# One core, two blocks: values fetched a token at a time and summed on TensorE in four column groups; experts in line by count, with small passes early

## The chip, the cores and the metric

One core of one Trainium2 chip. The metric is the device time of one execution in microseconds, median of the timed runs; the kernel before takes 2327.17 us (three runs, 2323.35 to 2337.86).

## What is computed

256 tokens of 1024 numbers go through two blocks. The first ends in a product-key layer: each of 8 heads picks 16 of 16384 experts for a token, so a token has 128 choices; each choice is one row of `expert_u` and one of `expert_v`.

```python
act = jax.nn.gelu(jnp.einsum('td,thkd->thk', xt, expert_u[idx]))
return jnp.einsum('thk,thkd->td', g * act, expert_v[idx])
```

The second block ends in a mixture of 32 experts, four for each token, with a swiglu of 1024 columns; gate_up is 1024 x 2048 and down 1024 x 1024 of f32 for each expert, 12 MB:

```python
gu = xb @ w_gate_up[e] + b_gate_up[e]
act = (up + 1.0) * gate * jax.nn.sigmoid(1.702 * gate)
return act @ w_down[e] + b_down[e]
```

## The kernel before, in words

**The product-key layer** (`peer`, from L752). A loop over 128 tiles of `expert_u` (L133) leaves `prods`, every token's product with every row, in SBUF; `topk_steps` finds rows, weights and indices meanwhile. Then, in an order written out by hand:

`hot(n)` (L848) and `chosen(n)` (L860) handle four tokens: four bf16 matmuls (L854) and two ACT steps make a one-hot, four f32 matmuls (L864) pick 128 columns of `prods`, and four DVE operations (L867) sum out the one that counts. `act` then has one column for each token, 128 choices down the partitions. `weigh(tb)` (L871) transposes a block of 128 tokens, takes the Gelu and multiplies with the gates, giving `w` with tokens down the partitions.

The values are fetched by choice: `fetch_pair` (L830, L836) asks on the GpSimd queue for two transfers of 512 KB, each the n-th value row of all 128 tokens of a block. One of a pair is scaled and added on DVE (L895), the other on TensorE by a diagonal of weights that ACT makes (`make_dg` L886, `use_pair` L898: two matmuls of 128x128 weights and 512 columns). Ten such buffers ("homes") exist, five pairs: the three `raw` buffers and the places of two older tiles.

The order (L900 to L920) is: choose all 32 groups of block 0, weigh block 0, and only then use pairs; each second pair is followed by one group of block 1. After that `prods` is given up, and a late part (L969) uses the other 64 pairs in five new homes, while it loads four tiles of `w_in_2`, splits them on DVE, and closes block 0. The three `raw` buffers take the mixer's first loads (L1013) then. `close_block` (L952) adds the DVE sum to the TensorE sum, transposes and updates the residual.

**The experts** (`second` L1324, `moe` L1403). Loads of 1 MB, eight of gate_up and four of down for each expert, go out on SP in the order of `ORDER` (L40) into 16 slots and three places used once; `refill` (L1380) sends the next as soon as the slot's earlier content has been used, so PE's progress frees slots. SP takes its instructions in order.

A pass (L1650) gives an expert up to 64 tokens (`CAP`). Tokens are gathered by a one-hot product (`gather` L1448), two experts at a time. `gate_up` (L1495) is, for each of eight chunks of 128 rows, four matmuls: weights are 128 x 64 (the tokens), 512 columns move, two halves of the output columns stand side by side in the array (`tile_position`). `swiglu` (L1504) runs on DVE and ACT, `turn` transposes, `down` (L1520) is four chunks of four matmuls, `combine` (L1535) adds rows back to the tokens by four matmuls. While pass e runs gate_up, the down of pass e-1 is put between its chunks. `combine` and the sums share four PSUM banks `acc`.

There are 33 passes: the 32 experts as numbered, and one for the second 64 tokens of the fullest expert, whose weights are loaded again through an address read by SP (`value_load` L1655, L1362). `rank_experts` (L1598) finds it. Passes beyond that stand in a conditional (L1729) that runs only if more tokens are left over.

## Time and profile before

| | |
|---|---|
| median of the timed runs | 2327.17 us |
| the profiled execution's own time | 2305.36 us |
| its span | 2303.7 us |
| busy, share of the span | PE 89%, weight loads 55%, DVE 44%, ACT 28%, POOL 32% |
| DMA | 709.29 MB, mean 308 GB/s |
| mean granted TensorE clock | 0.965 |

A row of the timeline gives the start, the busy time, the engine, the line, the operation, output from inputs, and the count; in brackets the idle time before it and who ended it. PE records each f32 matmul twice (its two halves), so eight records are four matmuls. PE is matmuls, PEld the loading of their weights, POOL GpSimd, SPq the queue of SyncE. The granted clock is a share of 2.4 GHz.

### The profile page before, as it was taken

To read this page: it belongs to the slowest core of one execution; us is meant where nothing else is said; L and a number is where in the kernel's file an instruction comes from. 1 tells how busy PE (TensorE), PEld (TensorE's weight loads), DVE (VectorE), ACT (ScalarE), POOL (GpSimd) and SP (SyncE) were. 2 spreads that over 40 slices of the span, in tenths; PEclk is the share of its full clock that TensorE was granted. 3 is DMA by queue.
4 is the path that set the end of the run, shared out by engine and by line. 5 is a ranking of instruction groups with operands and counts; after the bars stand their busy time and mean duration, and the time that the engine had idled before them with its cause. 6 is when DMAs were issued, how large, how long until landed. Compare 5 with 4: busy or idle time off the path is not lost. (4 is left out here: it accounts for less than half of the span.)

```text
span 2303.7 us, 29592 instructions
## 1 busy us (share of the span) xinstructions
PE 2043.3 (89%) x11552; PEld 1256.2 (55%) x11552; DVE 1020.3 (44%) x2271; ACT 640.0 (28%) x1113; POOL 728.3 (32%) x498
## 2 busy tenths in 40 slices
PE   3878898998999889966779899999999999989986
PEld 2777888998999744422257433344444333333332
DVE  5988879994111767757556211111111111111112
ACT  4554343554555833311112111111111011100101
POOL 7454566885555167757730000000000000000000
PEclk7989999999999999989999899999999999999998
DMA  8346632454554279999957699999999999999996
GB/s 327 110 164 230 263 130 88 171 191 170 183 187 165 74 260 406 398 376 397 402 212 279 251 382 420 395 420 382 420 420 420 420 420 420 420 420 420 420 420 260
DMA packets 117892, 709.29 MB, mean 308 GB/s; under 512 B 13776, under 2 KB 14032, under 8 KB 48368
## 3 DMA queue, kind: packets, MB, share of 16 engines
q1 hardware_dynamic: 78192, 564.96, 61.5%
q0 software_dynamic: 36864, 134.23, 15.2%
q10 hardware_dynamic: 2688, 8.12, 1.0%
q8 instruction: 93, 1.52, 0.3%
q14 instruction: 55, 0.45, 0.1%
HBM read 706.21 MB, written 1.05 MB: 307 GB/s over the span
## 5 line engine op out<-in xcount | busy, mean ns | idle before, releaser
L1499 PE MATMUL ps_gu<-w,hgs 128*64 128x512 f32 x2104 | 497.4, 600 | 18.9 <-DMA w<-in_w_gate_up 18.9
L1781 POOL TENSOR_TENSOR xT<-xT,ple_w 128x512 f32<-128x512 f32 x1 | 1.3, 1261 | 1010.9 <-ACT xT L1771 1010.9
L1499 PEld LDWEIGHTS ps_gu<-w,hgs 128*64 128x64 f32 x2104 | 139.8, 137 | 286.7 <-issue 218.9
L111 POOL TENSOR_TENSOR wsl<-raw,wsh 128x1024 fp32r<-128x1024 f32 x104 | 253.7, 2442 | 132.1 <-PE ps_a L133 97.5
L1527 PE MATMUL ps_y<-w,mid 128*64 128x512 f32 x1048 | 248.2, 595 | 16.5 <-DMA w<-in_w_down 15.9
L898 PE MATMUL acc<-vp,dg 128*128 128x512 f32 x344 | 173.7, 634 | 55.0 <-DMA vp<-in_v,rows_late 28.6
L1465 DVE TENSOR_SCALAR hgs<-ps_hg,cols 128x128 f32<-128x128 f32 (+1 forms) x68 | 27.6, 406 | 335.4 <-PE ps_hg L1455 317.6
L1527 PEld LDWEIGHTS ps_y<-w,mid 128*64 128x64 f32 x1048 | 73.5, 137 | 174.0 <-issue 149.1
L133 PE MATMUL ps_a<-h2h,wsh 128*128 128x256 f32 x1024 | 146.2, 286 | 15.3 <-ACT prods L804 15.3
L1506 DVE TENSOR_SCALAR mid<-ps_gu 128x512 f32<-128x512 f32 x33 | 22.7, 686 | 290.3 <-PE ps_gu L1499 290.3
L898 PEld LDWEIGHTS acc<-vp,dg 128*128 128x128 f32 x344 | 62.2, 199 | 155.1 <-issue 79.6
L133 PE MATMUL ps_a<-h2h,wsl 128*128 128x256 f32 x1024 | 145.3, 285 | 0.0
L836 POOL DMA_INDIRECT vp<-in_v,rows_late x118 | 127.6, 1082 | 53.8 <-issue 24.4
L133 PE MATMUL ps_a<-h2l,wsh 128*128 128x256 f32 x1024 | 144.6, 284 | 0.0
L133 PEld LDWEIGHTS ps_a<-h2h,wsh 128*128 128x128 f32 x1024 | 133.9, 194 | 15.9 <-ACT prods L804 15.9
L108 ACT CAST wsh<-raw 128x1024 fp32r<-128x1024 f32 x128 | 136.8, 1068 | 6.2 <-DMA raw<-in_uT 6.0
L133 PEld LDWEIGHTS ps_a<-h2h,wsl 128*128 128x128 f32 x1024 | 133.7, 194 | 0.0
L133 PEld LDWEIGHTS ps_a<-h2l,wsh 128*128 128x128 f32 x1024 | 133.0, 193 | 0.0
L804 ACT COPY prods<-ps_a 128x256 f32<-128x256 f32 x128 | 80.2, 627 | 175.7 <-PE ps_a L133 164.5
L867 DVE SCALAR_TENSOR_TENSOR junk_p<-iota_i,i1T,ps_ch 128x128 bf16<-128x128 f32 x256 | 89.0, 348 | 68.1 <-PE ps_ch L864 58.0
L836 POOL DMA_INDIRECT raw<-in_v,top x84 | 85.8, 1022 | 86.9 <-DVE vsum L893 52.9
L1463 ACT ACTIVATE hgs<-ps_hg,cols 128x128 f32<-128x128 f32 (+1 forms) x68 | 30.9, 454 | 286.2 <-DVE hgs L1465 286.2
(504 smaller groups left out, 3184.9 us busy)
## 6 DMA issues: line engine op xcount, KB each, us to landing
w<-in_w_gate_up SPq DMA_DIRECT2D x263, 1024.0 KB, 19.8
w<-in_w_down SPq DMA_DIRECT2D x131, 1024.0 KB, 19.8
raw<-in_uT SPq DMA_DIRECT2D x64, 1024.0 KB, 4.8
w_in<-in_w_in SPq DMA_DIRECT2D x25, 1024.0 KB, 7.1
wada<-in_w_ada SPq DMA_DIRECT2D x23, 1024.0 KB, 5.5
w_out<-in_w_out SPq DMA_DIRECT2D x8, 1024.0 KB, 5.0
w_query<-in_w_query SPq DMA_DIRECT2D x8, 1024.0 KB, 4.9
w_o_lru<-in_w_o_lru SPq DMA_DIRECT2D x4, 1024.0 KB, 5.3
```

Source lines behind the costliest of these rows:

```text
L108: nc.scalar.copy(out=hi, in_=src)
L111: lo.tensor_tensor(out=rest, in0=src, in1=hi.bitcast(F32), op=ALU.subtract)
L133: nc.tensor.matmul(ps, lhsT=a[:, c, :], rhs=b[:, c, :], start=first and m == 0, stop=last and m == 3 * n - 1)
L804: nc.scalar.copy(out=prods[:, :, i], in_=ps[:, :T])
L836: nc.gpsimd.indirect_dma_start(x[:, j], None, v_rows, bass.IndirectOffsetOnAxis(rows[:, tb, n:n + 1], 0))
L867: nc.vector.scalar_tensor_tensor(out=junk, in0=iota_i, scalar=o.i1[:, t:t + 1], in1=ps[:, r, :], op0=ALU.is_equal, op1=ALU.mult, accum_out ...
L898: nc.tensor.matmul(acc[2 * tb + f], lhsT=dg, rhs=x[:, 1, f * 512:(f + 1) * 512], start=n == 0, stop=n == NS - 2)
L1463: nc.scalar.activation(out=hg[:, c, :w], in_=ps[:, j, :], func=AF.Identity, scale=g, bias=b)
L1465: nc.vector.tensor_scalar(out=hg[:, c, :w], in0=ps[:, j, :], scalar1=g, scalar2=b, op0=ALU.mult, op1=ALU.add)
L1499: nc.tensor.matmul(p.pg[f][CAP * q:CAP * q + CAP], lhsT=p.hg[:, c, :], rhs=w[:, f * D + q * 512:f * D + (q + 1) * 512], start=False, stop= ...
L1506: nc.vector.tensor_scalar(out=g_s, in0=p.pg[0], scalar1=7.0, scalar2=None, op0=ALU.min)
L1527: nc.tensor.matmul(p.py[CAP * f:CAP * f + CAP], lhsT=ut[:, i, CAP * q:CAP * q + CAP], rhs=w[:, q * D + f * 512:q * D + (f + 1) * 512], sta ...
```

## The change

**Values.** A fetch now brings the 128 rows of one token (one row for each of its choices, down the partitions), still 512 KB. No transposed weights are needed: a group of four tokens, one of each quarter of a block (t, t+32, t+64, t+96), gets its weights as one 128x4 product on DVE, written into a zeroed tile so that four windows of 32 columns hold one weight column each at position g. Eight matmuls (32-column weights, four column groups of the array, two halves of 512 columns) add them into PSUM. Using starts after three chosen groups, and three groups are chosen for two used. There are twelve homes (the raw halves, two of the tag wsl, four halves of older tiles), late 14: the six raw halves stay, eight are new. The Gelu is taken on the chosen columns; indices and gates are transposed at the end of `topk_steps`. `close_block` copies instead of adding.

**Experts.** Experts 0 and 1 stay first; the other 30 are put in line by count by a new step on DVE, `line_up`: first the fullest (`TWIN`), then the 14 with the fewest tokens, then the rest. The small ones get 32 tokens and four column groups instead of two. The fullest gets 64 + 32 tokens from one set of loads: a second pass `second` uses the same chunk right behind the first. The 33rd pass is gone. SP reads each expert's number before its first load. The rows of the first four passes are kept and combined after pass 3, since `second` borrows their PSUM.

```diff
+FIXED = 2
+TWIN = FIXED
+SMALLS = 14
+BIG = TWIN + 1 + SMALLS
+SCAP = 32
...
+            def fetch(rows):
+                nonlocal n_fetched
+                while n_fetched < T and free_homes:
+                    t = order[n_fetched]
+                    n_fetched += 1
+                    fetched[t] = free_homes.pop(0)
+                    nc.gpsimd.indirect_dma_start(fetched[t], None, v_rows, bass.IndirectOffsetOnAxis(rows[:, t:t + 1], 0))
...
-            def weigh(tb):
...
+                x = four(act, n)
+                nc.scalar.activation(out=x, in_=x, func=AF.Gelu_apprx_tanh)
+
+            def use(n, columns):
+                x = cols_w[n % len(cols_w)]
+                columns(n, x[:, 31:].rearrange("p (r g) -> p g r", r=G)[:, 0, :])
+                tb, g = divmod(n, 32)
                 for f in range(2):
-                    nc.tensor.matmul(acc[2 * tb + f], lhsT=dg, rhs=x[:, 1, f * 512:(f + 1) * 512], start=n == 0, stop=n == NS - 2)
+                    for r in range(G):
+                        qs = slice(32 * r, 32 * r + 32)
+                        nc.tensor.matmul(
+                            acc[2 * tb + f][qs, :], lhsT=x[:, 32 * r + 31 - g:32 * r + 63 - g], rhs=fetched[order[n * G + r]][:, f * 512:(f + 1) * 512],
+                            start=g == 0, stop=g == 31, tile_position=(0, 32 * r),
+                        )
...
+            def weights(n, x):
+                nc.vector.tensor_tensor(out=x, in0=four(act, n), in1=four(o.g, n), op=ALU.mult)
...
+            AHEAD = 3
...
-            for n in range(n_hot // 2):
-                hot(n + 2)
-                chosen(n)
-            weigh(0)
...
+            pick(AHEAD)
+            q = 0
+            while picked < n_hot:
+                use(q, weights)
+                fetch(o.rows)
+                q += 1
+                pick(AHEAD + q * 3 // 2)
...
-            if e < NE:
+            if e < FIXED:
                 src = a["w_gate_up"][e, g] if g < 8 else a["w_down"][e, g - 8]
             else:
-                src = fullest(k.first_key, g)
+                if e not in k.expert_at:
+                    k.expert_at[e] = nc.sync.value_load(k.line[0:1, e:e + 1], min_val=0, max_val=NE - 1)
+                src = fullest(k.expert_at[e], g)
             nc.sync.dma_start(out=w, in_=src)
...
+        def products(self, lhsT, rhs, **flags):
+            for f in range(2):
+                for q in range(self.HALVES):
+                    at = f * D + q * self.n
+                    nc.tensor.matmul(self.pg[f][self.part(q), :self.n], lhsT=lhsT, rhs=rhs[:, at:at + self.n], tile_position=(0, self.SLOTS * q), **flags)
...
+    class Small(Pass):
+        HALVES, SLOTS = 4, SCAP
...
+        v.tensor_tensor(out=sq, in0=by_row(keys), in1=by_col(keys), op=ALU.is_gt)
+        v.tensor_reduce(out=rank, in_=sq, axis=AX.X, op=ALU.add)
...
+        v.tensor_tensor(out=sq, in0=by_row(rank), in1=by_col(at), op=ALU.is_equal)
+        v.tensor_tensor(out=tmp, in0=sq, in1=by_row(at), op=ALU.mult)
+        v.tensor_reduce(out=keys, in_=tmp, axis=AX.X, op=ALU.add)
+        v.tensor_copy(out=k.line, in_=keys[0:1])
+        for new, old in ((pos_l, k.pos), (gate_l, k.gate)):
+            for tb in range(NT):
+                v.tensor_tensor(out=tmp, in0=sq, in1=by_row(old[:, tb]), op=ALU.mult)
+                v.tensor_reduce(out=new[:, tb], in_=tmp, axis=AX.X, op=ALU.add)
...
-        for e in range(PASSES):
-            p = static(e) if e < NE else last
+        for e in range(NE):
+            p = static(e)
...
+                p.gate_up(c)
+                if twins:
+                    second.gate_up(c)
```

On TensorE in the value stretch, before: the last `hot` and `chosen` of a group, then two pairs (`acc` is the sum in PSUM, `raw` a home, `dg` the diagonal).

```order
L854 LDWEIGHTS ident_b
L854 MATMUL ps_i_8670<-i_3618,ident_b 128x128
L864 MATMUL ps_ch<-prods,hot 128x128 x4
L898 MATMUL acc_3625<-raw_3630,dg 128x512
L898 MATMUL acc_3626<-raw_3630,dg 128x512
L898 MATMUL acc_3625<-raw_3631,dg 128x512
L898 MATMUL acc_3626<-raw_3631,dg 128x512
```

The same place now (`cols_w` is the tile with the four weight columns, `raw` and `vp` two homes each).

```order
L867 LDWEIGHTS ident_b
L867 MATMUL ps_i_8011<-i_3618,ident_b 128x128
L877 MATMUL ps_ch<-prods,hot 128x128 x4
L895 MATMUL acc_3631<-raw_3637,cols_w_3624 32x512 x2
L895 MATMUL acc_3631<-vp,cols_w_3624 32x512 x2
L895 MATMUL acc_3632<-raw_3637,cols_w_3624 32x512 x2
L895 MATMUL acc_3632<-vp,cols_w_3624 32x512 x2
```

Two pairs are four fetches, half of them summed on DVE; now all four fetches of a group go through TensorE, in tiles of 32 weight columns.

On DVE in the same stretch, now: the sums of the chosen tokens (`junk_p`, four for each group) and the weights of the next used group (`cols_w`).

```order
L903 TENSOR_TENSOR cols_w_3623<-top_78 128x4
L880 SCALAR_TENSOR_TENSOR junk_p,top_78<-iota_i,i1T,ps_ch 128x128 x8
L903 TENSOR_TENSOR cols_w_3624<-top_78 128x4
L880 SCALAR_TENSOR_TENSOR junk_p,top_78<-iota_i,i1T,ps_ch 128x128 x4
L903 TENSOR_TENSOR cols_w_3625<-top_78 128x4
```

Each group's weights stand behind the sums of the one or two groups chosen just before; the 128x1024 sums of before are gone from this engine.

On SP at the start of the experts, now, with waits (`line` is the list of expert numbers).

```order
L1379 DMA w_10804<-in_w_gate_up 128x2048 [waits DMAHW1_49,PE_49]
L1377 TENSOR_LOAD line [waits DVE_49]
L1377 ISA x2
L1379 ISA
L1379 DMA w_10810<-in_w_gate_up 128x2048 [waits DMAHW2_49,PE_49]
L1379 ISA
L1379 DMA w_10825<-in_w_gate_up 128x2048 [waits DMAHW3_49,PE_49]
```

Before, the one such read stood one load earlier and waited for `rank_experts` alone; now it waits for the list, 29 more follow, each ahead of an expert's first load.

## Rows read from the trace of the kernel before

**Rows 1.** The page's slices, 40 of 57.6 us: what DMA moved.

```profile
GB/s 327 110 164 230 263 130 88 171 191 170 183 187 165 74 260 406 398 376 397 402 212 279 251 382 420 395 420 382 420 420 420 420 420 420 420 420 420 420 420 260
```

**Rows 2.** Windows: start:end length, busy us by engine, clock, DMA share, GB/s.

```profile
780.00:820.00 40.00, 32.05 (x232) 25.28 (x231) 29.63 (x161) 29.03 (x44) 1.87 (x2) 0.91 0.09 27
860.00:900.00 40.00, 36.50 (x157) 19.36 (x156) 27.68 (x72) 15.10 (x30) 30.55 (x32) 1.00 1.02 401
980.00:1020.00 40.00, 24.50 (x55) 10.19 (x54) 16.62 (x30) 4.65 (x12) 20.58 (x20) 0.77 1.02 414
1100.00:1140.00 40.00, 30.32 (x63) 10.33 (x61) 22.36 (x18) 6.97 (x17) 30.60 (x31) 1.00 1.02 407
```

**Rows 3.** POOL's timeline: last early fetch, first of the next.

```profile
758.53 0.94 POOL L836 DMA_INDIRECT vp<-in_v,top  x1 [0.31 <-issue]
812.38 0.94 POOL L836 DMA_INDIRECT raw<-in_v,top  x1 [52.91 <-DVE vsum L893]
```

**Rows 4.** PE's timeline in the value stretch and up to the mixer.

```profile
756.85 1.16 PE L864 MATMUL ps_ch<-prods,hot 128*128 128x128 f32 x8 [0.37 <-ACT hot L857]
...
883.03 0.39 PE L854 MATMUL ps_i<-i,ident_b 128*128 128x128 bf16 x4
883.25 1.11 PE L864 MATMUL ps_ch<-prods,hot 128*128 128x128 f32 x8
884.20 1.88 PE L898 MATMUL acc<-raw,dg 128*128 128x512 f32 x4
...
888.37 1.11 PE L864 MATMUL ps_ch<-prods,hot 128*128 128x128 f32 x8
...
997.61 3.75 PE L898 MATMUL acc<-raw,dg 128*128 128x512 f32 x4 [5.58 <-DMA raw<-in_v,top]
...
1180.27 0.66 PE L960 MATMUL ps_vT<-ident,vsum 128*128 128x128 f32 x4
...
1212.71 27.79 PE L1024 MATMUL ps_z<-xT,w_in 128*128 128x256 f32 x128
```

**Rows 5.** DVE's timeline: sums of chosen tokens; last row of hgs before the passes.

```profile
758.04 0.35 DVE L867 SCALAR_TENSOR_TENSOR junk_p<-iota_i,i1T,ps_ch 128x128 bf16<-128x128 f32 x1 [11.28 <-PE ps_ch L864]
...
759.68 0.35 DVE L867 SCALAR_TENSOR_TENSOR junk_p<-iota_i,i1T,ps_ch 128x128 bf16<-128x128 f32 x1
...
1297.60 0.41 DVE L1465 TENSOR_SCALAR hgs<-ps_hg,cols 128x128 f32<-128x128 f32 x1 [0.53 <-ACT hgs L1463]
```

**Rows 6.** Router product, 32-column tiles: PE's and PEld's timeline.

```profile
1282.59 1.13 PE L1267 MATMUL ps_l<-hT,rwg 128*32 128x256 f32 x16 [0.40 <-ACT hT L1262]
...
1283.08 0.16 PEld L1267 LDWEIGHTS ps_l<-hT,rwg 128*32 128x32 f32 x8 [0.33 <-ACT hT L1262]
```

**Rows 7.** First swiglu step of every pass (L1506), and windows of the expert stretch.

```profile
L1506 DVE TENSOR_SCALAR mid<-ps_gu x33: 680/691/692, 1316.6 to 2274.0; 128x512 f32<-128x512 f32 x33
...
1305.00:1560.00 255.00, 246.56 (x1226) 100.51 (x1224) 43.83 (x94) 29.19 (x60) 0.00 (x0) 1.00 0.98 401
1560.00:2263.00 703.00, 663.47 (x3290) 255.34 (x3287) 117.26 (x275) 71.03 (x154) 0.00 (x0) 1.00 1.01 418
```

**Rows 8.** PE's timeline, from 64-column tiles to transposes of 128.

```profile
1323.17 1.88 PE L1499 MATMUL ps_gu<-xT,hgs 128*64 128x512 f32 x8
1324.98 0.66 PE L1516 MATMUL ps_ut<-ident,mid 128*128 128x128 f32 x4
```

**Rows 9.** SP: the value read (L1655), the next loads; the page's loads of gate_up.

```profile
L1655 SPq TENSOR_LOAD <-keys_i x1: 460/460/460, 1299.5 to 1299.5; - x1
L1655 SPq FUSED_REGOPS  x1: 173/173/173, 1300.0 to 1300.0; - x1
...
1305.43 5.52 SPq L1363 DMA_DIRECT2D w<-in_w_gate_up  x4
...
w<-in_w_gate_up SPq DMA_DIRECT2D x263, 1024.0 KB, 19.8
```

**Rows 10.** DVE operations on 128x1024 (L120).

```profile
L120 DVE TENSOR_TENSOR wz<-w_in,wz x8: 1206/1223/1226, 1031.7 to 1106.6; 128x1024 fp32r<-128x1024 f32 x8
```

446 lines of the change are left out of this document (257 added, 189 removed).

## The prediction

> **What bounds the kernel now.** I read the page's slices first, then the windows of the stretches that the change touches, then the timelines of the engines inside them, and last what SP waits for. The slices show two stretches at the DMA limit, with an idle gap ahead of the first [rows 1]: slices 15 to 20 (value rows, near 400 GB/s) and 24 to 39 (expert weights, 420 GB/s). Between them lies the mixer, which the change leaves as it is.
>
> The value stretch. GpSimd issues a fetch in 0.94 us and the next 0.30 us later; after the tenth, at 758.5, it sits still for 52.9 us, until block 0 has its weights [rows 3]. In that time only the choosing runs, at one group of four tokens in 1.64 us, which is DVE's pace [rows 5]; the DMA share of 780 to 820 is 0.09 [rows 2]. From then on DMA is full (1.02) and a group of four tokens' values takes 5.12 us (chosen matmuls at 883.25 and 888.37), 1.28 us a fetch. The sums end at 1180.3, when the last transposes begin [rows 4].
>
> The expert stretch. The 33 swiglu steps start between 1316.6 and 2274.0, so a pass is 957.4/32 = 29.92 us. Twelve loads of 1.0486 MB in 29.92 us are 420.6 GB/s, and from 1560 on DMA gives 418 with a share of 1.01 [rows 7]: passes go at the speed of their weights, 2.49 us a load. From 1305 to 1560 DMA gives only 401: there PE (246.6 of 255 us busy) releases the slots late.
>
> **The sum is made against the profiled execution, 2305.4 us** (span 2303.7). The median of the timed runs is 2327.2, 0.9% above it, so I take the gain from the trace and subtract it from the median.
>
> **Part 1, values.** Removed: the wait for 32 chosen groups, 128 sums on DVE (not on the path while DMA was full), the 128 diagonals on ACT, half of PE's time for the sums (3.44 us of matmuls for four tokens become 1.72, below). Added: per group of four tokens one 128x4 product on DVE, one small Gelu on ACT, eight matmuls of 32 columns.
>
> Do four column groups run at once? The one place before with 32-column tiles is the router product: sixteen records of 256 columns, busy 1.13 us together, and the second eight began only at 1283.08, after ACT [rows 6]. One after the other they would take 8 x 0.43 = 3.4 us at the rate of the 128-column tiles (two 512-column products, four records, are over in 1.88 us at 884.20, so 0.86 each and a tail of 0.17 [rows 4]; 256 columns are half of that); two at a time 1.7. So four at a time, and the eight matmuls of a group should take 2 x 0.86 = 1.72 us.
>
> Start: the first chosen matmul stands at 756.85, as before. The third group's sums end near 758.04 + 3 x 1.64 = 763.0, and the first use follows. Twelve homes instead of ten keep POOL issuing until about 763 (two more at 1.24 us behind 759.5, and a wait for the last split's buffers), so the queue hardly runs dry: the 52.9 us are gone.
>
> What is late next is a chain, not DMA. The order of the engines is: use, choose one or two groups, next weights, next use; the weights of the next group stand on DVE behind the sums of the groups just chosen, and these stand on PE behind the use. For one round: use 1.72; hot to chosen 0.22 (883.03 to 883.25 [rows 4]); chosen to DVE's first sum 1.19 (756.85 to 758.04 [rows 4, 5]); 1.64 a chosen group, 1.5 of them on average, 2.46; the weights' product and the hand-over to PE 0.25, an estimate, below the 0.35 us of a DVE row over 128 columns since four need less; entering and leaving the 32-column tiles 0.15. Sum 6.0 us a round, against 5.12 that DMA and POOL need for four fetches. For 41 rounds 246 us: 763 + 246 = 1009.
>
> The price of entering another tile shape is in the trace for 64 columns: a chunk of gate_up starts at 1323.17, 1.72 us behind its forerunner, and the transposes of 128 columns, due at 1324.89, start at 1324.98 [rows 8]: 0.09 us, so about 0.15 for two changes. The Trainium skill (TensorEngine Tiling (Array Packing), Key Properties) says that a change of tiling mode drains TensorE, which speaks against this change: it mixes the two shapes twice in each round. The trace shows such a drain but a short one; by the rule at its worst (two drains as long as that tail of 0.17 us) the 41 rounds would cost 14 us instead of 6.
>
> After round 41, 92 tokens are left, 12 of them already asked for. 80 fetches at 1.28 are 102 us, the four w_in_2 loads (4.2 MB at 420) 10, the bias pieces 2: 1009 + 114 = 1123, and 4 us from the last landing to the last use. The sums end at 1127 instead of 1180: **-53 us**. The mixer's first three loads go out only now, because the raw buffers stay homes to the end; 3.1 MB are 7.5 us, and PE needs them at 1212.7, 32 us behind the sums' end [rows 4]; until then it works on weights that are there: no cost. If that cover were gone, it would cost 7.5.
>
> Ends: if DMA alone sets the pace, 244 fetches at 1.28 from 763, 12 for the loads, 4 at the end: 1091, -89. If only two column groups run at once, use is 3.44, a round 7.7, and 763 + 316 + 118 = 1197: +17. I stay at -53, since the router row is the nearest.
>
> **Part 2, experts.** The second helping of the fullest expert takes no weights of its own any more: 384 loads instead of 396. In a stretch that goes by loads, 12 x 2.49 = 30 us.
>
> The inputs decide whether a conditional pass is run: by the reference on them experts 0 and 1 have 32 and 33 tokens, the fullest of the others 70 (96 fit), the fourteen smallest 14 to 28 (32 fit), the rest at most 54. None is.
>
> Fourteen passes of 32 columns halve PE's part. Late, PE is busy 663.5 of 703 us [rows 7], 28.2 a pass; twelve chunks of 1.72 are 20.6 of it, all else 7.6. A small pass has twelve chunks of 0.86, 10.3, the 7.6, and up to 1.5 more for combine's eight products in place of four: some 19 us against 30 us of loads. So slots come free early, and 1305 to 1560 can go at 418 instead of 401: 255 x 17/418 = 10 us. The first three passes keep their PE time, and I take back 1.
>
> What is added at the start: line_up on DVE, thirteen operations on 1024 columns at the 1.22 us of the 128x1024 product [rows 10], 16 us, and 5 for small ones. The number that SP needs is ready after five of the thirteen, some 7.5 us after the last row of hgs (1297.60 + 0.41 [rows 5]), at 1305.5. SP issues its first load behind the value read at 1305.43 and waits for PE there anyway [rows 9]; the load that needs the number is the second, due at about 1307. Queued behind the read on SP are all further loads. I take 0; the end on the other side is 14 us, if it waits for the whole of line_up. The other 29 reads cost 0.46 + 0.17 us each [rows 9] on a queue whose loads land 19.8 us after issue, eight deep: hidden; without that cover 29 x 0.63 = 18 us. The first swiglu starts 3 us later behind line_up; the loads cover it.
>
> Sum **-39 us** (30 + 10 - 1); ends -47, if the stretch had no loss at all from 1290 on, and 30 - 14 - 18 = 2 less, so about 0.
>
> **Together -92 us: 2327 - 92 = 2235.** The ends added: -136 (2191) and +17 (2344).
>
> **Rivals.**
> DMA sets the pace of the values after all (the queues smooth the rounds of one and two groups, and a round's 6.0 falls to 5.2). For it: DMA held 1.02 before, with as much going on. Against: then DVE and PE worked on different pairs side by side, now they take turns. -89 - 39: 2199.
> Only two column groups at a time. For it: in the expert stretch four 64-column products take 1.72 us, two at a time [rows 8], and no long row shows more. Against: the router row. +17 - 39, 2305; a small pass would then take 29 us of PE, still under the loads.
> The experts gain nothing (reads and addresses from registers slow SP down): -53 alone, 2274. Against: the twelve loads by register of the last pass ran at the pitch of the others, and DMA stayed at 418 to the end of that stretch [rows 7].
> The clock falls, which would make it slower: PE has 3.5 us of work in a round of 6.0, 59%, and 64% in a small pass. The window from 980 with 24.5 of 40 us busy was granted 0.77, that from 1100 with 30.3 got 1.00 [rows 2]. If the new stretches ran at 1.2 GHz throughout, a round would be 9.0 us (+70 instead of -53), a small pass 38 us against 30 of loads (14 x 8.5 = +119, less 39): 2327 + 150 = 2477. It decides as soon as PE's work at the lower level exceeds 30 us a pass. Against: the busier PE is, the sooner the clock returns, and 0.77 came with a gap of 5.58 us at 997.6 [rows 4]; the new ones should be 2.6 us at most (1.64 + 1.19 + 0.25, less what PE has queued).
>
> **How the numbers follow.** My forecast 0.55 (its own range 2205 to 2265), DMA's pace 0.17, no gain at the experts 0.12, two groups 0.11, the clock 0.05. 2185 to 2290 leaves out the clock, most of the two-group case and little of the rest. A difference under 1%, 23 us, is about what a measurement cannot tell: faster 0.89 (all of the first three, half of the fourth), same 0.06, slower 0.05.
>
> **What would show it.** In the new profile: POOL without a gap of more than some 5 us behind its twelfth fetch; groups of chosen matmuls 4.9 and 6.6 us apart; sixteen 32-column records within 1.9 us; the sums' end near 1127; DMA at 415 or more from 30 us behind the first expert load on, with 384 loads; swiglu steps 29.9 apart from the fourth pass on. I am wrong if the 32-column records follow one another at 0.43 us, if SP stands at the first value read beyond 10 us, or if the late passes are no longer 29.9 us apart.

## The result: 1.2% slower, where 4% faster was forecast

The changed kernel takes 2355.1 us (median of 4 runs, 2350.3 to 2366.0) beside 2325.3 us of the kernel before (2322.4 to 2337.9): ratio 1.0121, 95% interval 1.0093 to 1.0149. Forecast were 2235 us, 2185 to 2290. Its profiled execution has a span of 2348.6 us.

On some chips (1, 4 and 9, "slowed" below: kernel before 2321 to 2344 us) kernels that fetch value rows by number run slower than on others (0, 10 and 15, "free": 2292 to 2300). For the first profile of before and for the timed runs of this section no chip is on record; by its time (2305) and its signals that profile, on which the prediction rests, is of the free kind, and by theirs the timed runs are of the slowed kind.

The page's slices of the changed kernel answer to [rows 1]: counted from 0, slices 14 to 18 of the value stretch move 237 to 304 GB/s where 400 were near (19 and 20, its late part, 393 and 376), and TensorE's clock has the digits 7 and 8 in 14 to 19.

```profile
PEclk7999999799999778788899989997888899999998
...
GB/s 321 108 198 252 250 73 144 108 168 194 193 181 169 248 247 282 237 273 304 393 376 171 314 288 287 382 416 420 420 420 419 419 420 421 420 420 420 420 420 253
```

The windows of the changed kernel (start:end length, busy us by engine, granted clock, DMA share, GB/s) answer to [rows 2, 7]. In 780 to 820 the DMA works now (0.71 where before had 0.09), as forecast; but it does not fill: 0.71 in 860 to 900 too, where before had 1.02. The experts begin 58 us later than before, so their first part is read 58 us later (1363 to 1618): 368 GB/s instead of 401, then 419.

```profile
780.00:820.00 40.00, 23.62 (x176) 12.44 (x176) 10.36 (x61) 10.27 (x21) 19.26 (x21) 0.83 0.71 251
860.00:900.00 40.00, 25.71 (x184) 11.71 (x185) 10.75 (x64) 11.53 (x23) 18.74 (x20) 0.82 0.71 245
980.00:1020.00 40.00, 23.18 (x190) 13.53 (x193) 13.30 (x78) 13.72 (x27) 21.65 (x24) 0.88 0.89 315
1100.00:1140.00 40.00, 22.38 (x109) 5.38 (x112) 11.43 (x39) 4.02 (x6) 24.05 (x26) 0.79 0.99 372
...
1363.00:1618.00 255.00, 222.68 (x1974) 112.10 (x1971) 50.64 (x128) 33.37 (x80) 0.00 (x0) 0.91 0.92 368
1618.00:2321.00 703.00, 614.03 (x4108) 270.35 (x4106) 101.60 (x251) 72.63 (x174) 0.00 (x0) 0.94 1.01 419
```

**A round that goes as forecast, and one that doesn't.** The timeline of the changed kernel, PE, ACT and DVE in order of time (start, us, engine, line, what; in brackets the idle time before it). Line 895 is the use, 867 the hot product, 877 the chosen product, 880 the sums; of before [rows 4, 5].

```profile
893.00 1.92 PE L895 MATMUL acc<-vp,cols_w 128*32 128x512 f32 x16 [2.18 <-DVE cols_w L903]
894.86 0.40 PE L867 MATMUL ps_i<-i,ident_b 128*128 128x128 bf16 x4
895.09 1.11 PE L877 MATMUL ps_ch<-prods,hot 128*128 128x128 f32 x8
...
895.29 0.69 ACT L869 ACTIVATE hot<-ps_i,minus_j 128x512 f32<-128x512 f32 x1 [2.18 <-PE ps_i L867]
...
896.24 0.35 DVE L880 SCALAR_TENSOR_TENSOR junk_p<-iota_i,i1T,ps_ch 128x128 bf16<-128x128 f32 x1 [3.29 <-PE ps_i L867]
...
897.92 1.92 PE L895 MATMUL acc<-raw,cols_w 128*32 128x512 f32 x16 [1.72 <-DVE junk_p L880]
899.77 0.40 PE L867 MATMUL ps_i<-i,ident_b 128*128 128x128 bf16 x4
900.01 1.11 PE L877 MATMUL ps_ch<-prods,hot 128*128 128x128 f32 x8
...
902.27 0.69 ACT L869 ACTIVATE hot<-ps_i,minus_j 128x512 f32<-128x512 f32 x1 [4.25 <-PE ps_i L867]
...
905.83 0.35 DVE L880 SCALAR_TENSOR_TENSOR junk_p<-iota_i,i1T,ps_ch 128x128 bf16<-128x128 f32 x1 [7.97 <-remote]
...
909.13 1.07 PE L895 MATMUL acc<-raw,cols_w 128*32 128x512 f32 x2 [6.84 <-DVE cols_w L903]
```

The first round takes 4.92 us (893.00 to 897.92), as forecast: sixteen records of 32 columns in 1.92 us, so four groups at once; ACT starts on the hot product 0.03 us behind its end, DVE on the chosen product 0.04 us behind its own. The second chooses two groups and should take 6.6; it takes 11.21. TensorE's records look the same, yet ACT starts 2.10 us behind the end of the hot product (900.17) and DVE 4.71 us behind the end of the chosen one (901.12). The ends of matmul records are modelled from their starts, so a delay inside TensorE shows only at those who wait for its semaphore. Set against the semaphore's own updates, 30 of the 61 chosen products with a signal between 774 and 1100 signal more than 0.3 us late; in the profile of before none of 62 does. I call these late signals. Some updates are missing from the traces, so the counts of late ones here and below are good to some ten products; a count of none is firm, every signal then comes within 0.02 us. The longest delay that a waiter shows is 5.46 us: DVE starts at 1046.85 on a product whose record ends at 1041.39. A lower clock alone is not enough for the delay: ACT and DVE start 3.56 us apart in the slow round (902.27, 905.83) and 0.95 in the other (895.29, 896.24), and half the clock would double 0.95.

The waits then cost the clock. In the windows of that round PE is idle from 906 to 909 and the granted clock is at its lower level, 1.2 of 2.4 GHz; the next use runs at it.

```profile
898.00:902.00 4.00, 4.00 (x39) 2.55 (x40) 0.00 (x0) 0.02 (x1) 3.08 (x4) 1.00 1.02 363
902.00:906.00 4.00, 0.29 (x3) 0.10 (x1) 0.17 (x1) 1.41 (x2) 2.21 (x3) 0.94 1.00 362
906.00:909.00 3.00, 0.00 (x0) 0.00 (x0) 2.68 (x17) 1.50 (x3) 0.00 (x0) 0.50 0.91 373
909.00:912.00 3.00, 2.87 (x16) 0.59 (x16) 0.08 (x1) 0.21 (x1) 0.00 (x0) 0.50 0.07 25
```

The Trainium skill (TensorE: Matmul & The Clock Gate, HAM oscillation — how this bites in real kernels) describes this: waits inside a loop let the clock fall, and each next step starts cold. The trace agrees: the use behind that wait takes from 909.13 to 912.62, 3.49 us instead of 1.92.

**Ahead of the values** a stall stands that the prediction did not have: PE waits 25.24 us for a copy in the middle of the products with u. The 128 copies of prods take 395.4 us from first to last start (367.0 to 762.4), 377.8 in the kernel before.

```profile
465.29 0.48 PE L753 MATMUL ps_ix<-ident,raw 128*128 128x128 f32 x1 [25.24 <-DVE i1T L754]
```

**At the experts** line_up begins at 1355.87 on DVE, and the first swiglu comes 21.3 us later; PE stands 5.32 us for it. SyncE waits only 2.8 us at the first value read (in before [rows 9] the read came early and the loads waited). In the stretch of the pass with the second helping the DMA share is 0.69, where before has 0.93 at the same stage (1342 to 1382); without the second helping (no_twin, below) it is 0.74 there. Timelines; SP's waits (us, times, longest); a window of the changed kernel and the same stage of no_twin; and the first swiglu step of the passes, as in [rows 7]:

```profile
1355.87 0.17 DVE L1663 COPY line_t<-keys 128x32 f32<-128x32 f32 x1
...
1377.19 0.67 DVE L1527 TENSOR_SCALAR mid<-ps_gu 128x512 f32<-128x512 f32 x1
...
1377.91 1.23 PE L1516 MATMUL ps_gu<-bgu,pick 96*64 96x512 bf16 x4 [5.32 <-DVE mid L1527]
```

```profile
SPq L1377 <- DVE line L1680: 2.8, 1, 2.8
```

```profile
1400.00:1440.00 40.00, 36.04 (x243) 15.36 (x238) 5.73 (x15) 4.39 (x10) 0.00 (x0) 0.91 0.69 260
```

```profile
1283.00:1323.00 40.00, 36.04 (x186) 16.21 (x182) 7.07 (x19) 5.89 (x13) 0.00 (x0) 0.91 0.74 290
```

```profile
L1527 DVE TENSOR_SCALAR mid<-ps_gu x32: 414/680/693, 1377.2 to 2318.6; 128x512 f32<-128x512 f32 x18, 128x256 f32<-128x256 f32 x14
```

**Where the time went.** Four stretches, read from the timelines: up to the first chosen product (line 877, formerly 864), from there to the end of the sums (895, formerly 898), to the first gather of rows for the experts (1471, formerly 1462), to the end of the span.

| us | forecast | free chips: before (first profile), changed (after_again) | slowed chips: before (before_again), changed |
|---|---|---|---|
| to the first chosen product | 0 | 756.8, 766.4: +9.6 | 756.5, 764.3: +7.8 |
| values | -53 | 423.5, 393.7: -29.8 | 453.3, 474.8: +21.5 |
| mixer | 0 | 108.0, 108.7: +0.7 | 108.8, 107.2: -1.6 |
| experts | -39 | 1015.3, 1000.3: -15.0 | 1016.0, 1002.3: -13.7 |
| sum | -92 | -34.5 | +14.0 |

The columns hold profiles, one for each kernel, and not medians: on chip 0 the timed medians are 23.5 us apart and not 34.5, in the result above +29.8 and not +14.0. Of the 106 us between -92 and +14, some 57 are missing on free chips too (23 of values, 24 of experts, 10 ahead of the values); some 49 are what a slowed chip takes more from the changed kernel than from the kernel before.

The rows for the first profile of the changed kernel (first and last start of a group; the sums end behind the last use):

```profile
L877 PE MATMUL ps_ch<-prods,hot x512: 274/275/582, 764.3 to 1099.7; 128*128 128x128 f32 x171
...
L895 PE MATMUL acc<-raw,cols_w x488: 589/617/1063, 774.7 to 1238.5; 128*32 128x512 f32 x163
...
L1471 PE MATMUL ps_hg<-disp,xhat x448: 274/275/582, 1346.3 to 2288.9; 128*128 128x128 f32 x118, 128*128 128x64 f32 x32
```

### The profile page after: what moved, and what is told of

The parts are those of the page before. It is cut to its first block, busy times and chain, and to the rows that moved or that the text cites. A ratio compares the mean times of both kernels' runs of the same rounds, so it can differ in the third digit from the quotient of the medians.

```text
span 2348.6 us, 34171 instructions
## 1 busy us (share of the span) xinstructions
PE 1914.0 (81%) x13592; PEld 1229.8 (52%) x13592; DVE 868.5 (37%) x2212; ACT 613.0 (26%) x1085; POOL 707.0 (30%) x501
## 5 line engine op out<-in xcount | busy, mean ns | idle before, releaser
L1516 PE MATMUL ps_gu<-w,hgs 128*32 128x256 f32 (+1 forms) x2936 | 407.9, 498 | 49.6 <-DMA w<-in_w_gate_up 49.3
L1516 PEld LDWEIGHTS ps_gu<-w,hgs 128*32 128x32 f32 (+1 forms) x2936 | 129.4, 126 | 259.7 <-issue 128.2
L1550 PE MATMUL ps_y<-w,mid 128*32 128x256 f32 (+1 forms) x1464 | 207.6, 507 | 44.3 <-DMA w<-in_w_down 43.4
L895 PE MATMUL acc<-raw,cols_w 128*32 128x512 f32 x488 | 121.0, 757 | 116.1 <-DVE cols_w L903 88.6
L1550 PEld LDWEIGHTS ps_y<-w,mid 128*32 128x32 f32 (+1 forms) x1464 | 68.3, 128 | 167.1 <-issue 107.9
L1527 DVE TENSOR_SCALAR mid<-ps_gu 128x512 f32<-128x512 f32 (+1 forms) x32 | 18.2, 570 | 307.1 <-PE ps_gu L1516 307.1
L1481 DVE TENSOR_SCALAR hgs<-ps_hg,cols 128x128 f32<-128x128 f32 (+1 forms) x56 | 22.2, 396 | 282.4 <-PE ps_hg L1471 267.9
L895 PEld LDWEIGHTS acc<-raw,cols_w 128*32 128x32 f32 x488 | 21.9, 125 | 180.6 <-DVE cols_w L903 93.3
L895 PE MATMUL acc<-vp,cols_w 128*32 128x512 f32 x344 | 78.1, 783 | 43.0 <-DVE cols_w L903 31.5
L116 POOL TENSOR_TENSOR wsl<-w_in,wsh 128x1024 fp32r<-128x1024 f32 x28 | 86.7, 3106 | 62.7 <-ACT wsh L113 62.5
```

The source lines that it names most:

```text
L116: lo.tensor_tensor(out=rest, in0=src, in1=hi.bitcast(F32), op=ALU.subtract)
L895: nc.tensor.matmul(acc[2 * tb + f][qs, :], lhsT=x[:, 32 * r + 31 - g:32 * r + 63 - g], rhs=fetched[order[n * G + r]][:, f * 512:(f + 1) * ...
L1481: nc.vector.tensor_scalar(out=hg[:, c, :w], in0=ps[:, j, :], scalar1=g, scalar2=b, op0=ALU.mult, op1=ALU.add)
L1516: nc.tensor.matmul(self.pg[f][self.part(q), :self.n], lhsT=lhsT, rhs=rhs[:, at:at + self.n], tile_position=(0, self.SLOTS * q), **flags)
L1527: nc.vector.tensor_scalar(out=g_s[:, :n], in0=self.pg[0][:, :n], scalar1=7.0, scalar2=None, op0=ALU.min)
L1550: nc.tensor.matmul(self.py[self.part(f), :self.n], lhsT=ut[:, c, self.part(q)], rhs=w[:, h * D + f * self.n:h * D + (f + 1) * self.n], sta ...
```

## The experiments

Two theories stood at the start. A: in every round TensorE idles for DVE's sums, the clock falls in these waits, and the lower clock lengthens the next round. B: TensorE itself is held back, by the four column groups or by the fetches.

### The two halves of the change

values_only: the choosing and the values of the changed kernel in the kernel before; experts_only: the reverse (whole functions exchanged).

> The values as in the changed kernel, the experts as in the kernel before. If the loss lies in the rounds of values alone: the sums end at 1235 to 1245 us as in the changed kernel (kernel before 1180), the rest takes 1123 us as in the kernel before, so 2355 to 2375 us, a ratio of 1.015 to 1.022, slower than the changed kernel itself. If the change of the experts loses too, the time is below the 2355 of the changed kernel.

> The experts as in the changed kernel, the values as in the kernel before. The prediction's step: 39 us less, 2265 to 2290 us, ratio 0.983. What the two traces say (from the end of the sums to the end 1123 us before, about 1110 after): 10 to 18 us less, 2307 to 2315 us, ratio 0.992 to 0.996. If the experts gain nothing: 2325.

On chip 4 values_only took 2380.3 us, ratio 1.0234 (1.0186 to 1.0282), a little over the range expected, experts_only 2320.0, 0.9949 (0.9929 to 0.9969). The loss is the values' alone; the experts gain 12 us, not 39, which is what the two traces said. The 2320.0 lies above the 2307 to 2315 of that reading, beside a kernel before at 2332.0 on this chip. What was not expected: the values of experts_only, the code of before unchanged, took 454.4 us, 31 more than in the profile of before, and 17 of 57 chosen products signal late. So late signals are not the changed kernel's own.

### Weights first

```
                 q += 1
+                ready(q, weights)
                 pick(AHEAD + q * 3 // 2)
```

(ready forms the weights of a use in its cols_w; the use then finds them there.)

> The changed kernel with one move: VectorE forms the weights of the next group ahead of the sums of the newly chosen groups, so that TensorE's next group waits for nothing that TensorE made in this round. Theory A (TensorE idles in every round for VectorE's sums, the clock falls in these waits, and the half clock makes the next round longer): rounds of 5.0 to 5.5 us, bound by GpSimd's four fetches of 1.25 us or the DMA, the last group chosen near 1000 us, 2245 to 2285 us in all. Theory B (TensorE itself is held back by the four column groups or by the fetches, whatever VectorE does: its signals come up to 4.6 us behind its records in some rounds): rounds stay above 7 us and the time above 2330.

2276.4 us on chip 4, ratio 0.9768 (0.9735 to 0.9801): 79 us below the median of the changed kernel above, and faster than either kernel. The values take 393.1 us instead of 474.8. Theory A's step is right: the order on DVE held TensorE up. But its rounds are 5.9 us, not 5.0 to 5.5 (781.7 to 1024.9 for 41), with the DMA at 344 GB/s, and 41 of 64 chosen products still signal late. B holds too, and it still costs: with the same order on a free chip (fixed_line and no_twin, below) the values take 351.0 and 353.7.

### What makes the signals late

no_fetch leaves out the fetches of the first part but twelve.

```
+                    if n_fetched > 12 and rows is o.rows:
+                        continue
```

> The changed kernel, but in the first part of the values only the first twelve rows are fetched; the later groups are summed from what lies there (the output is another one). Theory A: TensorE and VectorE hand over to each other as before, so the rounds stay at 7.5 to 8 us with the same falls of the clock, and the last group is chosen at 1085 to 1105. Theory B in the form that the fetches disturb TensorE: the late signals go, two-group rounds take 6.7 us at the full clock, the mean round is near 6, and the last group is chosen near 1010 to 1030.

Chip 4: 2283.3 us, ratio 0.9792 (0.9749 to 0.9834). Rounds of 4.9 and 6.53 us, 6.3 in the mean (778.0 to 1036.5 for 41), the last group chosen at 1033.8, late signals at 2 of 64, both at products that end before 772, while the twelve fetches run. That is near the prediction's round, on a slowed chip, with nothing but the fetches gone. B, in the form that the fetches disturb TensorE, is shown; A alone would have kept 7.5 to 8. A has a part in it all the same: 4.9 and 6.53 would give 5.7 in the mean, but 14 of the 21 rounds of one group take some 6.5, as their use runs at the lower clock for a part (3.23 us at 803.59, behind a wait of 2.17).

Four kernels then took the fetch apart on chip 1, one run each. before_again is the kernel before. plain_sp and plain_pool replace each fetch of the first part:

```
+                    if rows is o.rows:
+                        nc.sync.dma_start(out=fetched[t], in_=v_rows[P * (t % P):P * (t % P) + P])
+                        continue
```

(plain_pool: the same by nc.gpsimd); one_group turns the two loops of the use round:

```
-                for f in range(2):
-                    for r in range(G):
+                for r in range(G):
+                    for f in range(2):
```

> The kernel before, unchanged, profiled a second time. Its first profile (2305 us) lies below all of its timed runs (2323 to 2344). If TensorE's late signals belong to any kernel that fetches value rows while TensorE works, and were only absent from that one execution, this profile takes 2320 to 2340, its sums end near 1200 instead of 1180, and some signals of the chosen sums come more than 0.3 us behind their records. If they are the changed kernel's own, it takes 2305 again and no signal is late.

> The changed kernel, but in the first part of the values each fetch by row numbers is replaced by a plain transfer of as many bytes (128 fixed rows of 4 KB) on SyncE's queue, so other rows are summed. Theory B1 (the bytes that land in SBUF hold TensorE back): signals as late as in the changed kernel, the last group chosen at 1080 to 1110. Theory B2 (the fetches by row number, made on GpSimd, do it): rounds of 4.9 and 6.6 us as without fetches, the last group chosen at 1030 to 1045.

> As the kernel with plain transfers on SyncE's queue, but issued by GpSimd. Theory B1: the last group chosen at 1080 to 1110. If it is the list of row numbers that matters, near 1035 like the other; if it is that GpSimd issues them, near 1090 while SyncE's queue gives 1035.

> The changed kernel with the sixteen products of a round in another order: both halves of one group of columns, then the next group, so that at most two groups work at once. If the four groups at once (four streams of rows read from SBUF at a time) are what collides with the fetches, the late signals go, the sum of a round takes 3 to 5 us instead of 1.9, and the last group is chosen between 1060 and 1110. If the collision has nothing to do with the groups, signals stay late by up to 4 us and the longer sum is added: the last group chosen after 1140, 2390 us or more.

before_again took 2336.5 us; its sums end at 1209.9, 29.5 later than in the first profile, and 17 of 62 chosen products signal late. When they do follows the fetches within this one execution: from 763 to 810, while GpSimd stands still for 56 us, all 30 chosen products signal in time; the late ones lie ahead of it and behind it. GpSimd's first fetch behind its pause (as in [rows 3]):

```profile
814.30 0.94 POOL L836 DMA_INDIRECT raw<-in_v,top  x1 [55.99 <-DVE vsum L893]
```

Its windows, against [rows 2]:

```profile
860.00:900.00 40.00, 30.86 (x121) 15.81 (x120) 26.32 (x71) 11.96 (x24) 28.78 (x28) 0.96 0.88 316
980.00:1020.00 40.00, 29.77 (x111) 15.24 (x109) 19.41 (x50) 8.38 (x17) 26.34 (x26) 0.93 0.91 345
```

The 401 GB/s of [rows 2], on which the prediction stands, is 316 here: same kernel, same stretch.

plain_sp took 2284.0 and plain_pool 2279.3, the last group chosen at 1034.7 and 1032.6, no chosen product late. So it is neither the bytes nor GpSimd's queue (plain_pool's transfers and the fetches by number lie on the same queue, 144 packets for each 512 KB). A window of plain_pool, at 340 GB/s, where the changed kernel has 245:

```profile
860.00:900.00 40.00, 28.26 (x228) 16.39 (x225) 14.43 (x85) 15.64 (x29) 14.58 (x28) 0.91 0.91 340
```

The Trainium skill (DMA: Bandwidth & Descriptors, SWDGE vs HWDGE vs iDMA) says that GpSimd writes the descriptors of its transfers into SBUF, and that the queues of other engines don't pass there. By that alone plain_pool would be disturbed like the changed kernel; it isn't, so this does not explain it.

one_group took 2369.1 us, the last group chosen at 1122.8 and 26 of 60 chosen products late. That lies between what the two theories expected (1060 to 1110; after 1140). But its use did not take the 3 to 5 us expected: at the upper clock it still takes 1.95 (889.22 to 891.16), so the other order does not keep the groups apart, and this run does not test them.

```profile
889.22 0.63 PE L895 MATMUL acc<-raw,cols_w 128*32 128x512 f32 x2 [1.71 <-DVE cols_w L903]
...
890.56 0.60 PE L895 MATMUL acc<-vp,cols_w 128*32 128x512 f32 x2
```

Other runs settle it: before_again and experts_only have late signals without a 32-column product in their values, plain_sp and plain_pool have the four groups and none.

What is left is the fetch by number, or that its rows lie scattered.

```
+            seq = pool.tile([P, NT, P], I32, name="seq")
+            nc.gpsimd.iota(seq, pattern=[[0, NT], [P, P]], base=0, channel_multiplier=1)
+            seq = seq.rearrange("p b s -> p (b s)").bitcast(U32)
...
+                rows = seq if rows is o.rows else rows
```

> The changed kernel, but in the first part of the values the fetches by row number get fixed numbers: 128 rows that lie one behind the other, the same rows that the plain transfers took (other rows are summed). If GpSimd's fetch by row number is itself what holds TensorE back, signals stay late (over 0.3 us in a third or more of the chosen products), the last group is chosen at 1085 to 1105 and the time is 2340 to 2360. If it is that the rows lie scattered in memory, it behaves as the plain transfers: no late signal, the last group chosen near 1035, 2280 to 2290.

> The changed kernel with fixed, neighbouring row numbers in the first part of the values, once more, since the chip of the first try showed no late signals for scattered rows either, and so told nothing. It tells only where the kernel before takes 2320 or more beside it. Then: if GpSimd's fetch by number is itself the cause, a third or more of the chosen products signal late and it takes 2340 to 2360; if it is that the rows lie scattered, no signal is late and it takes 2270 to 2290, as with plain transfers of the same rows.

Both met free chips (15 and 10; kernel before 2293.3 and 2295.4): 2275.7 and 2279.0 us, no late signal. They tell nothing, since scattered rows make none there either. half_in_line uses the neighbouring numbers from the 88th fetch on, so that one execution holds both:

> The changed kernel; the first 88 tokens' rows are fetched by their real, scattered numbers, the rest of the first part by fixed, neighbouring numbers, with the same instruction. It tells only where the kernel before takes 2320 or more beside it. Then: if scattered rows are what it takes, late signals stand in the first twenty rounds (7.5 to 8.2 us a round) and are gone behind the 22nd group (6.0 to 6.4 us a round). If the fetch by number is enough, rounds stay at 7.5 to 8.2 us to the end. On an undisturbed chip both halves go at 6.2 to 6.4.

It met chip 9 (kernel before 2321.0) and took 2363.7 us. Its first fetch by fixed numbers is issued at 940.5. Late signals stand in both halves (12 of 30 chosen products before 930 us, 14 of 33 behind, up to the end), the rounds take 8.6 us up to the twentieth (171.5 for 20) and 8.0 from the 22nd to the 41st. Two windows, one of each half:

```profile
860.00:900.00 40.00, 23.14 (x152) 10.98 (x152) 10.37 (x61) 10.25 (x20) 14.98 (x16) 0.77 0.69 247
1040.00:1080.00 40.00, 21.74 (x164) 11.06 (x164) 8.90 (x53) 10.67 (x21) 16.28 (x19) 0.79 0.68 248
```

So the fetch by number is enough; scattered rows are not needed. How it reaches TensorE, and why only on some chips, stays open. That it is the chip, and not the hour, is the natural reading and not shown: only chip 9 was met at two times, slowed both times, with a free chip 10 between.

### How much is the changed kernel's own

> The changed kernel, unchanged, timed beside the kernel before and profiled again. If the late signals of TensorE belong to some executions or chips and not to a kernel: where the kernel before has none (its time near 2295 to 2305), the changed kernel has none either and takes 2270 to 2285, ratio 0.985 to 0.995; where the kernel before takes 2325 to 2335, the changed kernel takes 2350 to 2360 as it did, ratio 1.010 to 1.015. If they belong to this kernel, it takes 2350 or more in either case.

Chip 0, a free one: 2271.6 us beside 2295.2, ratio 0.9896 (0.9876 to 0.9915). The changed kernel is faster where the signals come in time, and slower where they don't. No chosen product is late. Rounds of two groups take 6.54 us, and rounds of one group 4.92 where the clock stays up; but 14 of the 21 rounds of one group take some 6.5. Its timeline, a round of two groups and a round of one at the lower clock; and two windows, a round of one group at the upper clock and that one:

```profile
892.10 0.40 PE L867 MATMUL ps_i<-i,ident_b 128*128 128x128 bf16 x4
892.33 1.11 PE L877 MATMUL ps_ch<-prods,hot 128*128 128x128 f32 x8
893.28 0.39 PE L867 MATMUL ps_i<-i,ident_b 128*128 128x128 bf16 x4
893.50 1.11 PE L877 MATMUL ps_ch<-prods,hot 128*128 128x128 f32 x8
896.78 3.15 PE L895 MATMUL acc<-vp,cols_w 128*32 128x512 f32 x16 [2.17 <-DVE cols_w L903]
...
903.31 1.07 PE L895 MATMUL acc<-raw,cols_w 128*32 128x512 f32 x8 [1.70 <-DVE cols_w L903]
```

```profile
885.32:890.24 4.92, 3.20 (x28) 1.58 (x29) 1.51 (x9) 1.64 (x4) 2.43 (x4) 1.00 0.91 323
896.78:903.31 6.53, 4.83 (x28) 2.07 (x29) 1.50 (x9) 1.62 (x4) 2.89 (x4) 0.74 0.92 341
```

From the use at 890.24 the round takes 6.54 us, with a wait of 2.17 on TensorE; the forecast had 6.6 and 2.6. The use at 896.78 runs at the lower clock for most of its 3.15 us, and its round has a granted clock of 0.74 in the mean. So theory A's loss stands on a free chip too: 14 rounds at 1.6 us are 23 us.

### The stall ahead of the values

The three transposes of block 0 go behind four heads of block 1, and all three ahead of the copies:

```
-        for j, (x, y) in enumerate(((idx[:, 0, :], out.i1), (row, out.rows), (odd, out.g))):
-            nc.tensor.transpose(ps[:, j * P:(j + 1) * P], x, k.ident)
-            nc.vector.tensor_copy(out=y[:, ts], in_=ps[:, j * P:(j + 1) * P])
...
+            if tb and h == 3:
+                yield from late_tail()
```

> The changed kernel with one move in the choosing ahead of the values: the three transposes of block 0 and the softmax that they need stand behind the first four heads of block 1, all three ahead of the copies. In the changed kernel TensorE stands 25.2 us in front of the second of these transposes. If that stall is on the path, the products with u last 378 to 381 us again instead of 395.5 (first to last copy), the values start 15 to 18 us earlier, and the time falls by as much against the changed kernel. If the time is taken up again later (the DMA or VectorE), it falls by less than 5 us.

Chip 0: 2257.9 us, ratio 0.9831 (0.9811 to 0.9851), 13.7 below the changed kernel, a little less than the 15 to 18 expected. The copies of prods take 379.6 us again, and the values begin at 753.6. The stall was on the path.

### Both moves

> The changed kernel with both moves: the weights of the next group ahead of the sums, and the three transposes later. The sum of both gains: 79 and 17 us less than the changed kernel where signals are late (2255 to 2262 beside a kernel before at 2325 to 2335, ratio 0.970), and 43 and 17 less where they are not (2205 to 2220 beside 2295 to 2305, ratio 0.963).

Chip 0: 2219.8 us (median of 5) beside 2295.2, ratio 0.9673 (0.9656 to 0.9689), the best of all; it is 51.8 below the changed kernel, where the two gains had been summed to 60. The values take 351.7 us. The DMA is full (share 1.03), and GpSimd issues one fetch right behind another (125 of them, busy 116.8 us with some 0.34 between two); which of the two sets the pace was not separated.

```profile
780.00:940.00 160.00, 155.05 (x1055) 72.94 (x1054) 67.50 (x398) 72.78 (x138) 116.81 (x125) 1.00 1.03 408
```

TensorE's records fill 155 of 160 us, the clock stays at its upper level, and the fetches run at 408 GB/s as in [rows 2]. On a slowed chip this kernel itself was not run, but its value stretch was, in short_line and short_no_twin below: 392.5 and 393.2 us, 41 more than here. So the late signals' price is about halved by weights first (81 us in the changed kernel), not gone.

### The experts

no_twin and fixed_line stand on weights_first, short_line and short_no_twin on both moves. The measure is the time from the first gather of rows to the end, 1015.3 in the kernel before, 1003.0 in weights_first (the 999.6 of two expectations had been taken otherwise) and 1002.4 in both. The same expert code takes 999.9 to 1004.9 in the other runs, so differences of 2 or 3 us say nothing.

```
no_twin
-                    second.gate_up(c)
...
-                second.combine(ys[3], cms[3])
fixed_line
-                src = fullest(k.expert_at[e], g)
+                src = a["w_gate_up"][e, g] if g < 8 else a["w_down"][e, g - 8]
short_line
-                v.tensor_tensor(out=tmp, in0=sq, in1=by_row(old[:, tb]), op=ALU.mult)
-                v.tensor_reduce(out=new[:, tb], in_=tmp, axis=AX.X, op=ALU.add)
+                v.tensor_copy(out=new[:, tb], in_=old[:, tb])
```

> The kernel with weights first, without the second helping of the fullest expert (its products, swiglu and combine are left out). In the kernel with weights first the passes take 999.6 us from the first gather of rows to the end, 12.5 less than in the kernel before, where 39 less were forecast. If TensorE's early passes (the double pass among them, some 17 us longer than a single one) hold the slots and starve the DMA, this falls by 12 to 17 us, to 983 to 988. If the loads set the pace there all the same, it falls by less than 4.

> The kernel with weights first, with the experts' weights loaded by fixed numbers: SyncE reads no number (the experts' weights then belong to others than the tokens' lists). If the thirty value reads and the addresses from registers cost the loads time, the 999.6 us from the first gather of rows to the end fall by 5 to 18 us; if they are hidden, as predicted, by less than 3.

> The kernel with both moves, with the second half of line_up cut: gates and places are copied instead of brought into the experts' order (eight operations of 1.22 us go, so tokens meet other experts). In the changed kernel line_up holds VectorE for 21.25 us ahead of the first swiglu, and TensorE stands 5.32 us for it. If the loads cover that stall, as predicted, the 1002.4 us from the first gather of rows to the end stay within 2 us. If the stall is on the path, since TensorE's early passes release the slots, they fall by 4 to 6 us.

> The same, and without the second helping of the fullest expert as well. If both prices add up, 1002.4 falls by 14 to 17 us, to 985 to 988, which is the 30 us of the twelve loads below the kernel before (1015.3): then the two early costs on TensorE are all that the prediction missed of these 30. If the loads set a floor, 991 to 993, as without the second helping alone (992.4).

fixed_line: 1002.1, 0.9 less, nothing beyond that scatter: the value reads are hidden. no_twin: 992.4, 10.6 less, a little under the 12 to 17 expected. short_line: 996.8, 5.6 less: the stall behind line_up is on the path. short_no_twin: 985.1, 17.3 less, so the two prices add up, and it is 30.2 below the kernel before: the twelve loads. Each of these is one run. (As whole times: 2223.7 and 2226.8 on chip 15, 2250.3 and 2239.4 on chip 9, the last two with late signals in the values.)

## Why the prediction was wrong, step by step

**The time that it subtracted from.** "The median of the timed runs is 2327.2, 0.9% above it, so I take the gain from the trace and subtract it from the median." This step failed first. The trace was, by its time and signals, of a free chip, the timed runs of slowed ones, and the gap of 22 us was not noise: the kernel before loses 30 us on a slowed chip, in the very stretch that was to be changed (before_again), and the changed one loses 81 there. The profile could have warned: 2305.4 lay below all timed runs, 2323.4 to 2337.9.

**The round of 6.0 us.** On slowed chips this is the term that failed: 8.0 us a round (774.7 to 1102.6 for 41), 82 us more than the 246 forecast. The chain that the prediction saw, use, choosing, sums, weights, next use, is there, and it is what makes the change sensitive: each late signal stands on it in full. The price of the late signals had no term. weights_first, which cuts the chain, takes 82 us off on a slowed chip (393.1 against 474.8) and 43 on a free one (351.0 in fixed_line, whose values are the same, against 393.7): the chain carries the loss in both cases, and what is left of the late signals costs some 42.

On a free chip 6.28 (772.5 to 1030.0 for 41), and 6.3 on a slowed one without fetches, lie close to 6.0, but partly by luck. The rounds of 4.9 and 6.6 that it named give 5.75 in the mean, not 6.0; measured are 4.92 and 6.54, so the sum was 0.27 too high for the upper clock, and the lower clock in 14 rounds, a term of nothing in the forecast, added 0.55. A drain between the two shapes beyond the 0.15 of the sum does not show in the 4.92.

**The clock**, a rival at 0.05, "If the new stretches ran at 1.2 GHz throughout". It did not fall throughout; it fell behind waits, to 0.79 to 0.88 in the windows of the changed kernel above, and to 0.88 in 860 to 900 on a free chip. The reason against it failed: it went by a gap of 5.58, and "the new ones should be 2.6 us at most" holds on a free chip (2.17), yet behind such waits of 2.17 the use ran at the lower level, for a part, in 14 of the 21 rounds of one group, 23 us in all. Nor do the rows bear out that "the busier PE is, the sooner the clock returns": in [rows 2] 32.05 us busy of 40 have 0.91, and 30.32 have 1.00. On a slowed chip the wait in the round shown is 6.84.

**The other rivals.** Two column groups at a time is out by the first round shown. The pace of the DMA (or of GpSimd's issuing) was not this kernel's, but it is that of both: 5.08 us a round (756.9 to 965.3 for 41), where DVE no longer takes turns with TensorE.

**The late part of the values**, 118 us from the last choosing to the sums' end, took 130.1 on a free chip (1030.0 to 1160.1). "12 of them already asked for" counted these rows as landed; in the timeline TensorE still waits for such rows (until 1037.6, 1040.2 and 1041.4), and twelve at 1.28 are 15 us. The term was 12 too small; no run took it apart. With 41 rounds at 0.28 too much, 11.5 us, this makes -53 into -29.5, and -29.8 was measured.

**"The first chosen matmul stands at 756.85, as before."** It did not: 764.3 and 766.4. The two transposes more in each block (row numbers and gates) put TensorE behind DVE's next block, for 25.2 us in one wait. I had read the diff there and not the order of DVE. tail_later, which takes the wait away, shows it. The products with u begin at different times as well (first copy at 366.2 to 376.6 in the other programs, 377.2 and 375.1 in before and before_again); why was not looked into.

**The experts, -39.** The 30 us of the twelve loads are there (short_no_twin). The value reads cost nothing, as said: the number was ready 7.8 us behind the last row of hgs (1355.54 + 0.41 to 1363.76), 7.5 forecast. Two steps failed. "The first swiglu starts 3 us later behind line_up; the loads cover it": line_up took its 21 us (1.22 an operation on 1024 columns, as [rows 10]), but the loads did not cover it: it cost 5.6 (short_line), as expected if TensorE's early passes release the slots. "The first three passes keep their PE time, and I take back 1": the second helping moved from the last pass to the third, and costs 10.6 to 11.7 there. With that the DMA stood at 0.69 in the stretch from which the prediction took another 10 us; they never came. -30 + 5.6 + 11 = -13.4, measured 10 to 15 less (1004.9 to 999.9).

**The signs it named.** The sixteen records came within 1.9 us, SyncE did not stand long; POOL stood 9.19 us behind its twelfth fetch instead of 5 at most, with its next fetch waiting for the first use (POOL's timeline, as [rows 3], where the gap was 52.9):

```profile
768.49 0.94 POOL L853 DMA_INDIRECT vp<-in_v,top  x1 [0.31 <-issue]
778.61 0.94 POOL L853 DMA_INDIRECT raw<-in_v,top  x1 [9.19 <-PE acc L895]
```

The steps from the eighth on are 30.5 us apart (1556.3 to 2318.6, 25 steps), not 29.9; the DMA gives 419 GB/s there at a share of 1.01, so the loads still set the pace.

## What to carry to other kernels

Look for the operation that an engine of the chain does last and needs least: here the next weights needed nothing of the round, and putting them ahead of the sums was worth more than the change itself. When a profile's own time lies outside the timed runs, take a second one before building a sum on it. A loop in which two engines take turns pays every disturbance in full, and again at TensorE's lower clock; with a round's slack between them it paid about half here (42 us instead of 81).

## What the runs showed that was not expected

Fetches by row number on GpSimd delay TensorE's semaphore signals by up to some 5 us on three of six chips, while its records look undisturbed; plain transfers of as many bytes, on the same queue, don't. It costs the value stretch of the kernel before 30 us and that of the changed one 81.

The delay is of one pattern: in the two-group rounds of the changed kernel that begin at 897.92, 928.87 and 1007.72, ACT starts on the hot product 4.35 to 4.37 us behind the start of the use instead of 2.29, and DVE on the chosen one 7.91 to 7.93 instead of 3.24.

Eight products of 32 columns by 512 in four groups take 1.92 us at the upper level and 3.64 at the lower (the uses at 897.92 and 1094.49 of the changed kernel); one after the other, at the 0.86 of a 512-column product, they would take 6.9 at the upper.
